# Second MLP: the lower part of the second of each two up weight tiles made by GpSimd

## The chip, the core and the metric

The kernel runs on one core of a Trainium2 chip. The metric is the device time of one execution in microseconds (us), from the core's first to its last instruction and what lies around that span; the median of several executions counts, and less is better.

The engines are named as the profile names them: PE is TensorE (matmuls), PEld its weight loads, DVE is VectorE, ACT is ScalarE, POOL is GpSimd, SP is the queue that issues the DMAs. SBUF is the on-chip memory in which all tiles lie, PSUM the banks into which matmuls accumulate.

## The reference

A trunk of two layers over 512 positions of width 1024, for one sequence, all in float32. Layer 0 is a hybrid attention mixer, layer 1 a pooling mixer; each is followed by a squared-ReLU MLP of inner width 4096, and the end is an RMSNorm. What matters here is the MLP of layer 1 and the end:

```
def squared_relu_mlp(h, w1, w2):
    return jnp.square(jax.nn.relu(h @ w1)) @ w2
...
x = x + (gate * squared_relu_mlp(h, mlp_w1[layer], mlp_w2[layer])).astype(x.dtype)
...
return rms_norm(x, final_norm_w)
```

## The kernel before, in words

**Products in parts.** Every float32 operand of a matmul is split into two parts of a shorter format: a high part (`wh`, `hh`, `gh`), which is the operand cast by ACT, and a lower part (`wl`, `hl`, `gl`), which is the operand less its high part, a subtract of 128 partitions. A product is then three matmuls (`mm3`, lines 368 to 372): high by high, high by lower, lower by high. So each weight tile is loaded by a DMA into a tile `w`, cast by ACT (line 364, `load_hi`) and subtracted (line 366). `load_hi` hands the subtract back as a function of the engine, and `load_w` calls it with its argument `lo`.

**The second MLP.** The inner width is worked through in eight chunks (0 to 7) of 512 columns, each as four blocks `f` of 128 columns. The generator `up_blocks` makes a chunk's blocks one after the other. For `f` = 0 and `f` = 2 it first loads two weight tiles of 128x1024 each: one for the first four of the eight slices of 128 rows of `w1` (`k0` = 0), one for the last four (`k0` = 4). A block is 24 matmuls of 128x512, three for each slice, in the order of the slices; two blocks share the two tiles. Then ACT takes relu and square from PSUM, and DVE makes the lower part of the result (line 418, `gl`, for a chunk of odd number). Chunk 0 and half of chunk 1 are made ahead; `up_blocks` makes the other half of chunk 1 and chunks 2 to 7, which is 13 pairs of tiles.

**Order.** Between the blocks stand the down products. Chunks are taken in pairs (0, 1), (2, 3), (4, 5) and multiplied with `w2` by a scheme of seven half-size products (class `Pair`: `begin`, `differences`, `steps`), whose sums and differences, and the splits of the `w2` tiles (lines 1606 and 1607), are work for DVE and ACT. The last pair (6, 7) is multiplied plainly (`direct`). In this part PE's order is the written one. That of ACT, DVE and POOL is decided by the scheduler when the program is built, unless the engine's name is bound to the wrapper `_InOrder`, which keeps each instruction behind those written before it. Once built, each engine runs its list in order.

Before the last blocks the engine name `V` (DVE) is bound anew:

```
V, weights = _InOrder(tc, nc.vector), []
for r in range(2):
    weights.append(pair.split(f"{r + 1}1"))
    next(blocks)
for _ in blocks:
    pass
```

At that point `blocks` is chunk 7 with its first block made. The loop splits four `w2` tiles (`split("11")`), makes block 1, splits four more (`split("21")`) and makes block 2, for which `up_blocks` first loads the last pair of weight tiles; then come block 3 and `direct`. The argument of `load_w` has a default, written before any of this:

```
def load_w(src, a, b, parts=1, lo=V, pool=None):
```

A default is bound where the function is defined: there, `V` is the engine without the wrapper.

Of the kernel before, what the change touches and what calls it, by code (L numbers as in the profile page):

```python
# [84 lines left out]
def trunk(ctx: ExitStack, tc: tile.TileContext, ins, out):  # L85
    nc = tc.nc
    V, S, G, TE = nc.vector, nc.scalar, nc.gpsimd, nc.tensor
# [20 lines left out]
    def mm_ps():  # L108
        return ps_mm.tile([P, 512], F32, tag="mm", name=nm("mm"))
# [230 lines left out]
    def load_w(src, a, b, parts=1, lo=V, pool=None):  # L340

        w, make_lo = load_hi(src, a, b, parts, pool)
        make_lo(lo)
        return w

    def load_hi(src, a, b, parts=1, pool=None):

        n = a * b
        rt = wraw.tile([P, RAW], F32, tag="raw", name=nm("w"))
        if parts == 1:  # L350
            load(rt[:, :n].rearrange("p (a b) -> p a b", a=a), src)
        else:
            dst = rt[:, :n].rearrange("p (a c b) -> p a c b", a=a, c=parts)
            for i in range(parts):
                load(dst[:, :, i], src[:, :, i])
        if pool is None:
            pool = wsplit
        if spare:
            turn[0] += 1
            if turn[0] % 6 >= 4:  # L360
                pool = spare[0]
        th = pool.tile([P, RAW], F32R, tag="wh", name=nm("wh"))
        tl = pool.tile([P, RAW], F32R, tag="wl", name=nm("wl"))
        S.copy(th[:, :n], rt[:, :n])  # L364
        w = tuple(t[:, :n].rearrange("p (a b) -> p a b", a=a) for t in (th, tl))
        return w, lambda e: e.tensor_tensor(tl[:, :n], rt[:, :n], th[:, :n].bitcast(F32), op=ALU.subtract)  # L366

    def mm3(ps, wh, wl, ah, al, start, stop):

        TE.matmul(ps, wh, ah, start=start, stop=False)  # L370
        TE.matmul(ps, wh, al, start=False, stop=False)  # L371
        TE.matmul(ps, wl, ah, start=False, stop=stop)  # L372
# [4 lines left out]
    class Mlp:  # L377
# [81 lines left out]
        def up_blocks(self, c, g, f0=0, pools=(None, None)):  # L459

            hh, hl = self.h
            for f in range(f0, 4):
                if f % 2 == 0:
                    by = []
                    for k0 in (0, 4):
                        c0 = c * FC + f * P
                        wh, wl = load_w(self.w1[:, k0 : k0 + 4, c0 : c0 + 256], 4, 256, pool=pools[f // 2])
                        by += [(wh, wl, i) for i in range(4)]
                ps = mm_ps()
                cs = slice(f % 2 * P, (f % 2 + 1) * P)  # L470
                for k in range(ND):
                    wh, wl, kk = by[k]
                    mm3(ps, wh[:, kk, cs], wl[:, kk, cs], hh[k], hl[k], k == 0, k == ND - 1)
                self.act(g, f, slice(0, T), ps)
                yield
# [129 lines left out]
    V, S, G, TE = [_InOrder(tc, e) for e in (V, S, G, TE)]  # L605
# [740 lines left out]
    V, S, G, TE = nc.vector, nc.scalar, nc.gpsimd, nc.tensor  # L1346
# [187 lines left out]
    V, S, G, TE = [_InOrder(tc, e) for e in (V, S, G, TE)]  # L1534
# [13 lines left out]
    V, S, G, TE = nc.vector, nc.scalar, nc.gpsimd, nc.tensor  # L1548
# [209 lines left out]
    TE, pools = _InOrder(tc, nc.tensor), (wsplit, wsplit2)  # L1758
# [27 lines left out]
    V, weights = _InOrder(tc, nc.vector), []  # L1786
# [43 lines left out]
```

## Time and profile before

| | |
|---|---|
| median of 3 executions | 1001.47 us (998.39 to 1001.85) |
| the profiled execution's own time | 997.38 us |
| its span, first to last instruction | 995.7 us |
| mean granted TensorE clock | 0.995 of full speed |
| PE busy | 968.0 us, 97% of the span |
| DVE busy | 675.7 us, 68% |
| ACT busy | 490.2 us, 49% |
| POOL busy | 188.0 us, 19% |

The profile is one execution. A row of the timeline gives an instruction's start and duration, and in brackets how long the engine had been idle before it and who ended that idle time. A row of a chain or a list of waits says who waited for whom. The part around the change runs from about 670 us to the last matmul at 987 us. Line numbers are those of the kernel before; L81 is the wrapper `_InOrder`, so every instruction issued through it has that line.

### The profile page before, as it was taken

To read this page: it belongs to the slowest core of one execution; us is meant where nothing else is said; L and a number is where in the kernel's file an instruction comes from. 1 tells how busy PE (TensorE), PEld (TensorE's weight loads), DVE (VectorE), ACT (ScalarE), POOL (GpSimd) and SP (SyncE) were. 2 spreads that over 40 slices of the span, in tenths; PEclk is the share of its full clock that TensorE was granted. 3 is DMA by queue.
4 is the path that set the end of the run, shared out by engine and by line. 5 is a ranking of instruction groups with operands and counts; after the bars stand their busy time and mean duration, and the time that the engine had idled before them with its cause. 6 is when DMAs were issued, how large, how long until landed. Compare 5 with 4: busy or idle time off the path is not lost.

```text
span 995.7 us, 14343 instructions
## 1 busy us (share of the span) xinstructions
PE 968.0 (97%) x5392; PEld 804.6 (81%) x5392; DVE 675.7 (68%) x1181; ACT 490.2 (49%) x913; POOL 188.0 (19%) x136
## 2 busy tenths in 40 slices
PE   6989999998999999999999999999999999999996
PEld 5568888788987778787777899998788788778885
DVE  3678886666886757666665427859557856886385
ACT  6566657665542433333343435665664544455511
POOL 0033436456120201111122345400000000000000
PEclk9999999999999999999999999999999999999999
DMA  9973566442375656465566312172451253042202
GB/s 309 339 173 106 170 188 217 154 141 64 107 240 183 221 157 214 134 208 187 170 211 207 107 49 83 60 245 78 127 169 43 85 161 93 0 152 102 74 34 84
DMA packets 119367, 145.57 MB, mean 146 GB/s; under 512 B 5782, under 2 KB 86018, under 8 KB 119298
## 3 DMA queue, kind: packets, MB, share of 16 engines
q1 hardware_dynamic: 119138, 144.59, 46.9%
q8 instruction: 42, 0.69, 0.3%
q14 instruction: 27, 0.22, 0.1%
q10 hardware_dynamic: 160, 0.07, 0.0%
HBM read 140.25 MB, written 4.39 MB: 145 GB/s over the span
## 4 chain that ended last, share of the span: by engine, by line
PE 87%; DVE 5%; issue 2%; DMA 2%; POOL 2%; ACT 1%; SPq 1%; DVEq 0%; POOLq 0%; ACTq 0%
PE mm L81 33%; PE mm L370 10%; PE sc L81 10%; PE mm L372 10%; PE mm L371 10%; PE po L81 5%; PE tp L81 5%; PE ad L81 2%; DMA adaw<-in_ada_w 1%; SPq L81 1%; DVE wl L1607 1%; POOL wl L81 1%; PE ad L283 1%; POOL sqsum L81 1%; DMA xin<-in_x 1%
## 5 line engine op out<-in xcount | busy, mean ns | idle before, releaser
L364 ACT CAST wh<-w 128x1024 fp32r<-128x1024 f32 x82 | 85.8, 1050 | 110.0 <-PE mm L371 80.2
L81 PE MATMUL mm<-hh,wl 128*128 128x512 f32 (+1 forms) x312 | 116.1, 379 | 2.0 <-DVE wl L366 2.0
L366 DVE TENSOR_TENSOR wl<-w,wh 128x1024 fp32r<-128x1024 f32 x76 | 100.0, 1320 | 24.3 <-ACT wh L364 23.2
L81 PE MATMUL mm<-hh,wh 128*128 128x512 f32 (+1 forms) x312 | 116.3, 380 | 0.0
L81 PE MATMUL mm<-hl,wh 128*128 128x512 f32 (+1 forms) x312 | 115.5, 377 | 0.0
L81 POOL TENSOR_TENSOR wl<-w,wh 128x1024 fp32r<-128x1024 f32 x36 | 87.6, 2444 | 79.9 <-ACT wh L81 77.1
L371 PE MATMUL mm<-hl,wh 128*128 128x512 f32 (+1 forms) x256 | 95.7, 376 | 0.0
L372 PE MATMUL mm<-hh,wl 128*128 128x512 f32 (+1 forms) x256 | 95.5, 375 | 0.0
L370 PE MATMUL mm<-hh,wh 128*128 128x512 f32 (+1 forms) x256 | 94.3, 377 | 0.0
L1606 ACT CAST wh<-w 128x512 fp32r<-128x512 f32 x100 | 56.9, 619 | 53.2 <-PE po L81 21.9
L370 PE MATMUL mm<-gh,wh 128*128 128x512 f32 x192 | 75.9, 395 | 0.0
L371 PE MATMUL mm<-gl,wh 128*128 128x512 f32 x192 | 74.8, 390 | 0.0
L372 PE MATMUL mm<-gh,wl 128*128 128x512 f32 x192 | 74.8, 390 | 0.0
L81 PEld LDWEIGHTS mm<-hh,wl 128*128 128x128 f32 x312 | 58.7, 188 | 15.6 <-DVE wl L366 4.0
L81 PEld LDWEIGHTS mm<-hh,wh 128*128 128x128 f32 x312 | 58.9, 189 | 11.6 <-ACT wh L364 0.6
L81 PEld LDWEIGHTS mm<-hl,wh 128*128 128x128 f32 x312 | 58.9, 189 | 11.3
L1607 DVE TENSOR_TENSOR wl<-w,wh 128x512 fp32r<-128x512 f32 x84 | 54.7, 689 | 17.7 <-ACT wh L1606 17.5
L248 DVE SCALAR_TENSOR_TENSOR acc<-adaw,sc,acc 128x512 f32<-128x512 f32 x60 | 46.7, 778 | 21.0 <-DMA adaw<-in_ada_w 20.4
L274 POOL TENSOR_TENSOR adaw<-adaw 128x512 f32<-128x512 f32 x12 | 15.7, 1306 | 232.4 <-ACT adaw L272 199.4
L375 DVE SCALAR_TENSOR_TENSOR x<-mm,mod,x 128x512 f32<-128x512 f32 x48 | 35.7, 746 | 31.8 <-PE mm L372 31.8
L81 ACT CAST wh<-w 128x1024 fp32r<-128x1024 f32 (+1 forms) x44 | 43.8, 1004 | 25.8 <-DMA w<-in_attn_w_in 9.3
L372 PEld LDWEIGHTS mm<-hh,wl 128*128 128x128 f32 x256 | 48.2, 188 | 9.6 <-issue 0.8
(499 smaller groups left out, 2488.9 us busy)
## 6 DMA issues: line engine op xcount, KB each, us to landing
w<-in_mlp_w SPq DMA_DIRECT2D x98, 512.0 KB, 4.1
adaw<-in_ada_w SPq DMA_DIRECT2D x92, 512.0 KB, 4.6
w<-in_mlp_w SPq DMA_DIRECT2D x64, 256.0 KB, 3.7
w<-in_attn_w_in SPq DMA_DIRECT2D x8, 512.0 KB, 3.6
w<-in_attn_w_out SPq DMA_DIRECT2D x8, 512.0 KB, 3.5
w<-in_attn_w_in SPq DMA_DIRECT2D x8, 392.0 KB, 7.9
xin<-in_x SPq DMA_DIRECT2D x4, 512.0 KB, 5.7
adaw<-in_ada_w SPq DMA_DIRECT2D x8, 256.0 KB, 6.1
```

What stands on the lines that cost most here:

```text
L81: return lambda *args, **kw: self.tc.keep_in_program_order(f(*args, **kw))
L248: V.scalar_tensor_tensor(acc, rv, sk, acc, op0=ALU.mult, op1=ALU.add)
L274: G.tensor_tensor(rv[:, 0], rv[:, 0], rv[:, 1], op=ALU.add)
L283: TE.matmul(ps[32 * j : 32 * j + 32], one_col[:, 31 - r : 63 - r], self.acc[:, j * P : (j + 1) * P], start=True, stop=True)
L364: S.copy(th[:, :n], rt[:, :n])
L366: return w, lambda e: e.tensor_tensor(tl[:, :n], rt[:, :n], th[:, :n].bitcast(F32), op=ALU.subtract)
L370: TE.matmul(ps, wh, ah, start=start, stop=False)
L371: TE.matmul(ps, wh, al, start=False, stop=False)
L372: TE.matmul(ps, wl, ah, start=False, stop=stop)
L375: V.scalar_tensor_tensor(x[j][:, ts], ps, g, x[j][:, ts], op0=ALU.mult, op1=ALU.add)
L1606: S.copy(th[:, cs], self.raw[key, f])
L1607: V.tensor_tensor(tl[:, cs], self.raw[key, f], th[:, cs].bitcast(F32), op=ALU.subtract)
```

## The change

For the second MLP (`pairs` is set there and only there) `up_blocks` hands the subtract of the pair's second tile to POOL; that of the first stays on DVE.

```
@@ -464,7 +464,8 @@
                     by = []
                     for k0 in (0, 4):
                         c0 = c * FC + f * P
-                        wh, wl = load_w(self.w1[:, k0 : k0 + 4, c0 : c0 + 256], 4, 256, pool=pools[f // 2])
+                        lo = G if k0 and self.pairs else V
+                        wh, wl = load_w(self.w1[:, k0 : k0 + 4, c0 : c0 + 256], 4, 256, lo=lo, pool=pools[f // 2])
                         by += [(wh, wl, i) for i in range(4)]
```

The lists of PE, ACT and SP keep their order; DVE's is 13 rows shorter and POOL's 13 longer. The places of which the prediction speaks follow. A name's last number tells one tile from another; from line 467 on a line of the changed kernel has a number one higher.

POOL, end of its list, in the changed kernel: the first 6 of 13 new rows, which stand behind all that POOL had before (its last row of work was a sum `sqsum`, at 647 us).

```order
L366 TENSOR_TENSOR wl_1112_6927<-w_1110_6924,wh_1111_6926 128x1024
L366 TENSOR_TENSOR wl_1154_7189<-w_1152_7186,wh_1153_7188 128x1024
L366 TENSOR_TENSOR wl_1174_7340<-w_1172_7337,wh_1173_7339 128x1024
L366 TENSOR_TENSOR wl_1202_7472<-w_1200_7469,wh_1201_7471 128x1024
L366 TENSOR_TENSOR wl_1228_7634<-w_1226_7631,wh_1227_7633 128x1024
L366 TENSOR_TENSOR wl_1264_7848<-w_1262_7845,wh_1263_7847 128x1024
```

Each is a subtract that stood in DVE's list; POOL has nothing else between them.

DVE at the first pair of chunk 4 (tiles 7842 and 7848), before; `sum0`, `sum1` and `x4` take up products of the pair (2, 3), `sl` is the lower part of a difference that PE multiplies next, `gp` belongs to the block's result.

```order
L1640 TENSOR_TENSOR sum0_6835<-sum0_6835,sc_1253_7805 128x512
L366 TENSOR_TENSOR wl_1261_7842<-w_1259_7839,wh_1260_7841 128x1024
L1640 TENSOR_TENSOR sum1_6836<-sum1_6836,sc_1254_7818 128x512
L1621 TENSOR_TENSOR sl_1256_7834<-gf_1148_7179,sh_1255_7833 128x1024
L366 TENSOR_TENSOR wl_1264_7848<-w_1262_7845,wh_1263_7847 128x1024
L430 TENSOR_TENSOR gp_1257_7837<-gf_1258_7838,gp_1257_7837 128x256
```

In the changed kernel the same place of DVE's list reads:

```order
L1641 TENSOR_TENSOR sum0_6835<-sum0_6835,sc_1253_7805 128x512
L366 TENSOR_TENSOR wl_1261_7842<-w_1259_7839,wh_1260_7841 128x1024
L1641 TENSOR_TENSOR sum1_6836<-sum1_6836,sc_1254_7818 128x512
L1622 TENSOR_TENSOR sl_1256_7834<-gf_1148_7179,sh_1255_7833 128x1024
L430 TENSOR_TENSOR gp_1257_7837<-gf_1258_7838,gp_1257_7837 128x256
```

Tile 7848 is gone from DVE, and nothing else has moved.

DVE at the end of chunk 7, before: the last pair's tiles are 8901 and 8907; `gl_1404` is the lower part of chunk 7's result, from block 0 (`r_1428`) and block 1 (`r_1434`); the other `wl` are the splits of `w2`.

```order
L366 TENSOR_TENSOR wl_1441_8901<-w_1439_8898,wh_1440_8900 128x1024
L366 TENSOR_TENSOR wl_1444_8907<-w_1442_8904,wh_1443_8906 128x1024
L418 TENSOR_TENSOR gl_1368_8497<-r_1402_8746,gh_1367_8496 128x512
L418 TENSOR_TENSOR gl_1404_8769<-r_1428_8839,gh_1403_8768 128x512
L81 TENSOR_TENSOR wl_1430_8845<-w2_1405_8770,wh_1429_8844 128x512
...
L81 TENSOR_TENSOR gl_1404_8769<-r_1434_8881,gh_1403_8768 128x512
L81 TENSOR_TENSOR wl_1436_8887<-w2_1409_8778,wh_1435_8886 128x512
...
L81 TENSOR_TENSOR wl_1438_8893<-w2_1412_8784,wh_1437_8892 128x512
L81 TENSOR_TENSOR gl_1404_8769<-r_1446_8935,gh_1403_8768 128x512
```

In the changed kernel the same place reads:

```order
L418 TENSOR_TENSOR gl_1368_8497<-r_1402_8746,gh_1367_8496 128x512
L418 TENSOR_TENSOR gl_1404_8769<-r_1428_8839,gh_1403_8768 128x512
L81 TENSOR_TENSOR wl_1430_8845<-w2_1405_8770,wh_1429_8844 128x512
...
L81 TENSOR_TENSOR gl_1404_8769<-r_1434_8881,gh_1403_8768 128x512
L81 TENSOR_TENSOR wl_1436_8887<-w2_1409_8778,wh_1435_8886 128x512
...
L81 TENSOR_TENSOR wl_1438_8893<-w2_1412_8784,wh_1437_8892 128x512
L81 TENSOR_TENSOR wl_1441_8901<-w_1439_8898,wh_1440_8900 128x1024
L81 TENSOR_TENSOR gl_1404_8769<-r_1446_8935,gh_1403_8768 128x512
```

Tile 8907 has gone to POOL. Tile 8901, which stays on DVE, has moved down behind both splits and behind block 1's `gl`: `V` is now read inside `up_blocks` when the pair is loaded, and there it is the wrapped engine (its row has L81). On PE block 2 of chunk 7 reads tile 8901 with its third matmul, right behind block 1.

## Rows read from the trace of the kernel before

**Rows 1.** The page's first part: engine, busy us, share of span, instructions.
```profile
PE 968.0 (97%) x5392; PEld 804.6 (81%) x5392; DVE 675.7 (68%) x1181; ACT 490.2 (49%) x913; POOL 188.0 (19%) x136
```

**Rows 2.** Who PE waited for, 560 to 996 us: total, times, longest.
```profile
PE mm L81 <- DVE wl L366: 2.0, 4, 0.5
...
PE mm L81 <- DVE gl L418: 0.7, 3, 0.2
```

**Rows 3.** Line 366 over the span: duration ns min/median/max, first and last start.
```profile
L366 DVE TENSOR_TENSOR wl<-w,wh x76: 1209/1223/2325, 266.4 to 920.5; 128x1024 fp32r<-128x1024 f32 x76
...
L366 POOL TENSOR_TENSOR wl<-w,wh x6: 2394/2402/2409, 538.3 to 566.4; 128x1024 fp32r<-128x1024 f32 x6
```

**Rows 4.** Timeline of POOL and DVE, 245 to 251 us: start, duration, instruction.
```profile
245.67 7.63 POOL L81 TENSOR_TENSOR wl<-w,wh 128x1024 fp32r<-128x1024 f32 x3
...
246.31 2.20 DVE L81 SCALAR_TENSOR_TENSOR hl<-ht,mod,hh 128x256 fp32r<-128x256 f32 x1 [0.32 <-ACT hh L81]
```

**Rows 5.** Timeline of PE, ACT and DVE, 917 to 937 us.
```profile
917.73 1.23 DVE L366 TENSOR_TENSOR wl<-w,wh 128x1024 fp32r<-128x1024 f32 x1 [2.16 <-ACT wh L364]
...
931.15 0.40 PE L81 MATMUL mm<-hh,wl 128*128 128x512 f32 x1
...
931.70 0.59 ACT L415 ACTIVATE r<-mm 128x512 f32<-128x512 f32 x1
...
933.64 0.69 DVE L81 TENSOR_TENSOR gl<-r,gh 128x512 fp32r<-128x512 f32 x1 [3.30 <-ACT r L417]
...
934.25 2.49 DVE L81 TENSOR_TENSOR wl<-w,wh 128x512 fp32r<-128x512 f32 x4
```

**Rows 6.** Windows: us, busy us (instructions) of PE, PEld, DVE, ACT, POOL, PEclk, DMA.
```profile
914.00:988.00 74.00, 73.40 (x329) 60.05 (x327) 44.13 (x78) 25.83 (x53) 0.00 (x0) 1.00 0.16 54
...
229.00:230.00 1.00, 0.00 (x0) 0.00 (x0) 0.00 (x0) 0.61 (x3) 0.92 (x2) 1.00 0.04 14
...
231.00:232.00 1.00, 1.00 (x3) 0.82 (x4) 0.11 (x1) 0.00 (x0) 1.00 (x1) 0.50 0.07 16
...
234.00:235.00 1.00, 1.00 (x9) 1.00 (x9) 0.96 (x3) 0.13 (x1) 0.00 (x0) 0.91 0.67 132
```

**Rows 7.** Timeline of DVE and PE, 675 to 697 us: chunk 1, tile 6927.
```profile
675.31 1.22 DVE L366 TENSOR_TENSOR wl<-w,wh 128x1024 fp32r<-128x1024 f32 x1
...
687.46 0.69 DVE L1607 TENSOR_TENSOR wl<-w,wh 128x512 fp32r<-128x512 f32 x1 [0.40 <-ACT wh L1606]
...
695.71 0.69 DVE L418 TENSOR_TENSOR gl<-r,gh 128x512 fp32r<-128x512 f32 x1
...
696.46 0.50 PE L81 MATMUL mm<-wh,gl 128*128 128x512 f32 x1 [0.24 <-DVE gl L418]
```

**Rows 8.** Timeline at tile 7189 (chunk 2) and at tile 7848 (chunk 4).
```profile
711.65 0.50 PE L81 MATMUL mm<-hh,wl 128*128 128x512 f32 x1 [0.53 <-DVE wl L366]
711.85 1.05 ACT L364 CAST wh<-w 128x1024 fp32r<-128x1024 f32 x1
...
795.67 1.04 ACT L364 CAST wh<-w 128x1024 fp32r<-128x1024 f32 x1
...
795.95 0.50 PE L81 MATMUL mm<-hh,wl 128*128 128x512 f32 x1 [0.53 <-DVE wl L366]
796.41 1.22 DVE L1621 TENSOR_TENSOR sl<-gf,sh 128x1024 fp32r<-128x1024 f32 x1
```

**Rows 9.** Timeline at tiles 8507 and 8660 (first and second pair of chunk 6).
```profile
880.13 1.05 ACT L364 CAST wh<-w 128x1024 fp32r<-128x1024 f32 x1
...
880.87 0.69 DVE L1755 TENSOR_TENSOR sum<-x,sum 128x512 f32<-128x512 f32 x1
...
883.89 0.50 PE L81 MATMUL mm<-hh,wl 128*128 128x512 f32 x1 [0.41 <-DVE wl L366]
...
901.66 3.13 ACT L364 CAST wh<-w 128x1024 fp32r<-128x1024 f32 x3 [1.36 <-PE po L81]
...
902.82 0.40 PE L81 MATMUL mm<-hh,wh 128*128 128x512 f32 x1
```

More of the change, by code (lines that the diff above doesn't have):

```diff
@@ L466, in up_blocks @@
                         c0 = c * FC + f * P
-                        wh, wl = load_w(self.w1[:, k0 : k0 + 4, c0 : c0 + 256], 4, 256, pool=pools[f // 2])
+                        lo = G if k0 and self.pairs else V
+                        wh, wl = load_w(self.w1[:, k0 : k0 + 4, c0 : c0 + 256], 4, 256, lo=lo, pool=pools[f // 2])
                         by += [(wh, wl, i) for i in range(4)]
```

## Prediction

> **What bounds the kernel now.** The page's first part comes first [rows 1]: PE is busy 97% of the span, POOL 19%. The windows narrow that to the stretch of the change: from 914 to 988 us PE is busy 73.40 of 74 us, and the rest is the end, after its last matmul [rows 6]. So the path that sets the end runs through PE, and a change there counts only by what it does to PE's waits. The list of waits shows how little there is to win: from 560 us on PE waits 2.0 us for line 366, in four pieces of at most 0.5, and 0.7 us for line 418 [rows 2]. If the change took away every one of these, it would give 2.7 us, 0.3% of the time, and a measurement of this kernel can't tell less than about 0.5% (5 us) from no change. What it can cost has no such lid: a tile that comes late stops PE for as long as it is late.
>
> **What the change takes and adds.** Thirteen subtracts of 128x1024 go from DVE to POOL. On DVE one takes 1.22 us and on POOL 2.40 us, both medians over whole groups [rows 3]. DVE loses 13 x 1.22 = 15.9 us of work, POOL gains 13 x 2.40 = 31.2 us in a stretch where it had none: its last such subtract began at 566.4 us [rows 3]. No matmul, cast or DMA is added or moved. POOL frees a raw tile some 1.2 us later than DVE did, and the load that goes into it is issued that much later; each such load feeds a cast some 10 us away or more, so I cost that at nothing (without that cover, 1.2 us a time).
>
> Two things decide what this does to PE: when the second tile is ready, and whether DVE can work beside POOL.
>
> **DVE beside POOL.** In the timeline from 245.67 us POOL has three such subtracts in a row, 7.63 us for 3 x 2.40 = 7.20 [rows 4]. The first ends near 248.07. DVE starts an instruction with two SBUF operands at 246.31, of a quarter of the elements, and it takes 2.20 us, to 248.51 [rows 4]: it got nowhere until POOL was done. So I count a POOL subtract as 2.40 us in which DVE can't do that kind of work, and POOL as waiting for the end of such a DVE instruction if that came first. The Trainium skill (SBUF — State Buffer, section "Who interferes with whom") speaks against the change here: a VectorE instruction with two SBUF inputs and a GpSimd instruction that reads SBUF shut each other out for the whole instruction, whichever comes first. The trace agrees, with the 2.20 us above.
>
> **Seven places where the second tile, or DVE, comes late.** A block's matmuls start 0.233 us apart in the timeline, 24 in 5.60 us (over 914 to 988 us it is 73.40 us for 329 recorded ones, 0.223, a few of them smaller [rows 6]). A block's third matmul is the first to read a lower part, and the one that reads the second tile's comes 12 later, 12 x 0.233 = 2.80 us. I allow 0.08 us from the cast's end to POOL and 0.05 from POOL's end to PE.
>
> - Tile 7189: PE took up the first tile at 711.65, so it wants the second at 714.45. The cast ends at 711.85 + 1.05 = 712.90 [rows 8]; POOL runs from 712.98 to 715.38, PE goes on at 715.43. **1.0 us.**
> - Tile 7848: wanted at 795.95 + 2.80 = 798.75. The cast ends at 796.71, but DVE holds an instruction with two SBUF operands from 796.41 to 797.63 [rows 8]; POOL from 797.63 to 800.03, PE at 800.08, against about 798.8 now. **1.2 us.** Were POOL not held up, 799.24, or 0.4.
> - Tile 8507: PE takes it at 883.89 now, after 0.41 us of waiting. The cast ends at 881.18, a DVE instruction at 881.56 [rows 9]; POOL to 883.96. **0.1 us**, or 1.2 if DVE's next instruction gets in first.
> - Tile 8660: block begun at 902.82, wanted 14 x 0.233 = 3.27 us later, at 906.09. Its cast is the second of the three from 901.66, ended by 903.75 [rows 9]; DVE, which takes the first tile when the first of these casts is done (902.71), holds POOL up to about 904.0; POOL to 906.4. **0.4 us.** The same pattern, three casts in a row, stands in chunks 2 and 4; there it gives 0.3 each. **0.6 us.**
> - Tile 6927 is in time (PE wants it over 3 us later), but here DVE is the late one. It works almost without a break from this subtract at 675.31 to the `gl` at 695.71 that PE waits for at 696.46; the one pause is 0.40 us [rows 7]. It loses 2.40 us to POOL, saves the 1.22, and has 0.40 of slack. **0.8 us.**
> - The other six second tiles are wanted 5 us or more after POOL can have them, and where POOL stands in DVE's way DVE is idle for 3 us soon after: nothing.
>
> Together 1.0 + 1.2 + 0.1 + 0.4 + 0.6 + 0.8 = **4.1 us**. If the two engines could work side by side, it would be 1.0 + 0.4 - 0.2 (tile 8507 sooner than now) + 0.2 + 0.5 + 0 = 1.9; if DVE got in first at tile 8507, 5.2. These are the bounds. By the skill's rule it is the 4.1, without it the 1.9.
>
> **The tile that moved: the largest term.** The order of DVE's list shows something that the words of the change don't say. The first tile of the last pair, 8901, is still DVE's, but it is now issued through the wrapper that keeps the written order, behind both splits and behind the `gl` of chunk 7's block 1. Before, DVE did it at 917.73, long ahead; PE reads it at 931.15 [rows 5]. In the new order it must wait for that `gl`, which waits for ACT's activations of block 1. These can't start until block 1 is done; they begin at 931.70, and `gl` at 933.64 [rows 5]. Four split subtracts follow, from 934.25, 0.60 us apart [rows 5]; the fifth in line is tile 8901, from 936.65 to 937.87. PE goes on near 937.93. **PE stands still for 6.8 us.** Nothing covers it: PE's list has only two more matmuls ahead of that one, and all that is late afterwards hangs on PE. From there to the last matmul PE has no pause that could take the delay up [rows 6], so it reaches the end whole. I see no bound that lets it shrink by more than the few tenths between instructions.
>
> **The clock.** In the row for 229 to 230 us PE did nothing, and in that for 231 to 232 its granted clock is 0.50, the lower level of 1.2 GHz in place of 2.4; at 234 to 235 it is back at 0.91 [rows 6]. So a pause of under 3 us was followed by about 3.2 us at half speed. After one of 6.8 us I expect the same: 3.2 us at half speed lose **1.6 us**; the bounds are 0 and 3.2 (twice as long).
>
> **The sum.** 4.1 + 6.8 + 1.6 = 12.5 us slower. The profiled execution took 997.38 us, 1.7 outside its span of 995.7, so it would take 1009.9. It was faster than the median of 1001.47 by 4.1 us, and the median is what counts: 1001.47 + 12.5 = **1014.0 us**.
>
> **The rivals.**
> - Only the moved tile counts: POOL's tiles come in time after all, because casts earlier in ACT's list or shorter gaps give them the lead that they lack. For it: four of the seven places are under half a microsecond. Against it: at 711.65 and 795.95 the second cast ends only 1.5 and 2.0 us before the tile is wanted, and POOL takes 2.40. Time: 1001.47 + 6.8 + 1.6 = 1009.9 us.
> - Not slower: the moved tile finds cover. That is so if DVE reaches it by 931.15 us, 6.8 earlier than in my count, which needs the `gl` ahead of it not to hang on block 1. For it: from 914 to 988 us DVE is idle 40% of the time [rows 6]. Against it: the printed order, and the activation at 931.70. Then only the seven places are left, 1.9 to 4.1 us: 1003.4 to 1005.6 us, which a measurement doesn't tell from no change.
> - The relief of DVE wins: 15.9 us fewer, all 2.7 us of waits gone, nothing late: 998.8 us. Against it: at 711.65 and 795.95 PE waits for a pair's first tile, 0.53 us each [rows 8], and that tile's way through ACT and DVE is unchanged.
>
> That the change doesn't do what it says is excluded by POOL's list, which has the thirteen rows.
>
> **How the numbers follow.** The forecast (moved tile, late POOL tiles, clock) has 0.75, its own range being 6.8 + 1.9 to 6.8 + 5.2 + 3.2 over the median, 1010 to 1017. Only the moved tile: 0.13. Not slower: 0.09. Relief: 0.03. Faster by over 0.5% would need more than relief can give, save for the spread of the runs: 0.03. Within 0.5%: the third case and a piece of the relief: 0.09. Slower by over 0.5%: 0.88. The range goes down to 1005, which takes in the second case measured against the fastest run shown (998.39 + 6.8 = 1005.2), and up to 1018, a us more than the first, for the spread of the runs.
>
> **What would show it.** In the new profile: a wait of PE for DVE's `wl` of L81 of 6 to 7 us, near 940 us, the DVE row before it being four splits; granted clock 0.50 for a few microseconds just after; waits of PE for POOL's `wl` of L366 of about 1 us at the first pair of chunks 2 and 4; DVE instructions of twice their length beside POOL's. I am wrong if that long wait is missing (the third rival), or if PE's waits for POOL add up to under 1 us (the first).

## The result, and the profile after

The changed kernel takes **1014.79 us** (median of 4 runs, 1014.24 to 1016.06); the kernel before, on the same chip, 1001.29 us. The ratio is 1.0149, with a 95% interval of 1.0127 to 1.0171: 1.5% slower. The predicted time was 1014.0 us. The profiled execution of the changed kernel took 1014.97 us, its span was 1013.2 us.

The page's first part after the change, against [rows 1]:

```profile
PE 974.2 (96%) x5392; PEld 807.6 (80%) x5392; DVE 671.8 (66%) x1168; ACT 490.0 (48%) x913; POOL 222.0 (22%) x149
```

POOL has 13 instructions more and 34.0 us more work, DVE 13 instructions fewer and only 3.9 us less. Thirteen subtracts of 1.22 us would be 15.9: much of the other 12 us is DVE instructions drawn out beside POOL (rows below have 4.11 us in place of 1.89, and 3.42 in place of 1.22). The busy share of an engine hides this: it counts the waiting as work. Both differences are rough to some 2 us: e2 below, in which both engines do exactly the work of the kernel before, has 678.0 and 185.9 us for DVE and POOL, where the kernel before has 675.7 and 188.0.

Who PE waited for from 560 us on, against [rows 2] (total, times, longest):

```profile
PE mm L81 <- DVE wl L81: 6.7, 1, 6.7
PE mm L81 <- POOL wl L366: 2.5, 6, 0.9
PE mm L81 <- DVE wl L366: 1.6, 3, 0.5
PE mm L81 <- DVE gl L418: 1.3, 3, 0.8
PE po L81 <- DVE hl L81: 0.9, 1, 0.9
```

Two lines are new: one wait of 6.7 us, and six for POOL. The wait for `gl` has grown by 0.6 us, and of four waits for DVE's line 366 three are left. The last line stands in the list before too, with the same numbers. The long one, in the timeline of PE, ACT and DVE from 937 to 947 us, against [rows 5]:

```profile
939.12 0.40 PE L81 MATMUL mm<-hl,wh 128*128 128x512 f32 x1
939.94 0.59 ACT L415 ACTIVATE r<-mm 128x512 f32<-128x512 f32 x1
...
941.88 0.69 DVE L81 TENSOR_TENSOR gl<-r,gh 128x512 fp32r<-128x512 f32 x1 [3.34 <-ACT r L417]
942.50 3.62 DVE L81 TENSOR_TENSOR wl<-w,wh 128x512 fp32r<-128x512 f32 x5
...
946.17 0.79 PE L81 MATMUL mm<-hh,wl 128*128 128x512 f32 x1 [6.65 <-DVE wl L81]
```

After two matmuls of block 2 PE stands still, at 939.12 + 0.40. DVE itself is idle for 3.34 us, until ACT has made block 1's result; then come `gl` and five subtracts, which the view shows as one row. Four of them are the splits of `w2`, the fifth is tile 8901, for which PE waits. The windows of one microsecond around it (us, busy us and instructions of PE, PEld, DVE, ACT and POOL, then PEclk, the granted clock, and the DMA):

```profile
940.00:941.00 1.00, 0.00 (x0) 0.00 (x0) 0.00 (x0) 0.97 (x3) 0.00 (x0) 1.00 0.00 0
941.00:942.00 1.00, 0.00 (x0) 0.00 (x0) 0.12 (x1) 0.82 (x2) 0.00 (x0) 0.75 0.00 0
942.00:943.00 1.00, 0.00 (x0) 0.00 (x0) 1.00 (x2) 0.00 (x0) 0.00 (x0) 0.50 0.00 0
...
950.00:951.00 1.00, 1.00 (x3) 0.74 (x3) 0.00 (x0) 0.00 (x0) 0.00 (x0) 0.50 0.00 0
951.00:952.00 1.00, 1.00 (x4) 0.83 (x3) 0.00 (x0) 0.00 (x0) 0.00 (x0) 0.63 0.00 0
952.00:953.00 1.00, 1.00 (x6) 0.78 (x6) 0.00 (x0) 0.00 (x0) 0.00 (x0) 1.00 0.00 0
```

The clock falls to 0.50, 1.2 GHz, during the pause, and it is still there when PE is at work again. A row between the levels is a mean: 0.63 says that the low level filled 0.74 of that microsecond, so it ended near 951.74. (The x of a window counts every matmul that has a part in it, 3 to 4 there and later 6; fewer begin in it.) The pace is read from PE's timeline:

```profile
946.76 0.63 PE L81 MATMUL mm<-hh,wh 128*128 128x512 f32 x1
...
951.46 0.53 PE L81 MATMUL mm<-hh,wl 128*128 128x512 f32 x1
```

Between these two starts lie eleven steps, so a step takes 4.70 / 11 = 0.427 us, where 0.233 is usual at the full clock. A microsecond of work at the low clock therefore loses 1 - 0.233 / 0.427 = 0.45 us.

The other places, each in PE's timeline:

```profile
701.36 0.50 PE L81 MATMUL mm<-wh,gl 128*128 128x512 f32 x1 [0.79 <-DVE gl L418]
...
719.20 0.39 PE L81 MATMUL mm<-hl,wh 128*128 128x512 f32 x1
720.29 0.50 PE L81 MATMUL mm<-hh,wl 128*128 128x512 f32 x1 [0.70 <-POOL wl L366]
720.62 0.39 PE L81 MATMUL mm<-hh,wh 128*128 128x512 f32 x1
...
742.82 0.50 PE L81 MATMUL mm<-hh,wl 128*128 128x512 f32 x1 [0.18 <-POOL wl L366]
...
806.18 0.50 PE L81 MATMUL mm<-hh,wl 128*128 128x512 f32 x1 [0.90 <-POOL wl L366]
...
828.74 0.50 PE L81 MATMUL mm<-hh,wl 128*128 128x512 f32 x1 [0.19 <-POOL wl L366]
...
891.66 0.50 PE L81 MATMUL mm<-hh,wl 128*128 128x512 f32 x1 [0.39 <-POOL wl L366]
...
914.20 0.50 PE L81 MATMUL mm<-hh,wl 128*128 128x512 f32 x1 [0.18 <-POOL wl L366]
```

The three rows around 720 us show how to price a wait. From the start of one matmul to the start of the second after it takes 720.62 - 719.20 = 1.42 us, where two steps of 0.233 are usual: 0.95 us lost, of which the list calls 0.70 a wait. A new wait costs some 0.26 us more than its entry in the list, since that counts from the end of the matmul before (its row overlaps the next one's) and the first matmul behind the pause is slower.

**A ledger that leaves out what differs ahead of the change.** How long the kernel takes up to chunk 1 differs from run to run: the matmul that waits for `gl` there starts at 696.46 us in the trace before [rows 7], at 701.36 in this one, at 696.77 to 702.47 in the others. All but the wait itself arose before the change acts. So I compare what comes behind: from the start of that matmul to the end of the span, plus what its own wait has grown. Each row rests on one profiled execution; e3 and e6, where nothing but that wait should differ, come within 0.1 us of it.

| kernel | start | span | rest | change of rest, with the wait at the start |
|---|---|---|---|---|
| before | 696.46 | 995.7 | 299.2 | |
| the change | 701.36 | 1013.2 | 311.8 | +12.6 + 0.55 = **+13.2** |
| e1, POOL only | 698.31 | 1000.8 | 302.5 | +3.3 + 0.55 = **+3.8** |
| e2, moved tile only | 700.90 | 1008.6 | 307.7 | **+8.5** |
| e3, six late tiles | 700.27 | 999.4 | 299.1 | **-0.1** |
| e4, filled pause | 700.79 | 1010.3 | 309.5 | +10.3 + 0.55 = **+10.8** |
| e5, ahead of the split | 702.47 | 1011.0 | 308.5 | +9.3 + 0.55 = **+9.8** |
| e6, tile 6927 only | 701.05 | 1000.3 | 299.2 | 0.0 + 0.56 = **+0.6** |
| e7, halves | 696.77 | 994.5 | 297.7 | **-1.5** |
| e8, the change again | 698.84 | 1010.6 | 311.8 | +12.5 + 0.56 = **+13.1** |

The prediction's sum was 12.5.

### The profile page after: what moved, and what is told of

Its sections match the earlier page's. It is cut to its first block, busy times and chain, and to the rows that moved or that the text cites. A ratio compares the mean times of both kernels' runs of the same rounds, so it can differ in the third digit from the quotient of the medians.

```text
span 1013.2 us, 14351 instructions
## 1 busy us (share of the span) xinstructions
PE 974.2 (96%) x5392; PEld 807.6 (80%) x5392; DVE 671.8 (66%) x1168; ACT 490.0 (48%) x913; POOL 222.0 (22%) x149
## 5 line engine op out<-in xcount | busy, mean ns | idle before, releaser
L81 PE MATMUL mm<-hh,wl 128*128 128x512 f32 (+1 forms) x312 | 118.1, 386 | 10.8 <-DVE wl L81 6.7
L81 PE MATMUL mm<-hh,wh 128*128 128x512 f32 (+1 forms) x312 | 117.5, 384 | 0.0
L81 PE MATMUL mm<-hl,wh 128*128 128x512 f32 (+1 forms) x312 | 116.9, 382 | 0.0
L366 POOL TENSOR_TENSOR wl<-w,wh 128x1024 fp32r<-128x1024 f32 x19 | 49.4, 2606 | 275.5 <-ACT wh L364 171.8
L81 POOL TENSOR_TENSOR wl<-w,wh 128x1024 fp32r<-128x1024 f32 x36 | 87.3, 2434 | 82.7 <-ACT wh L81 76.9
L366 DVE TENSOR_TENSOR wl<-w,wh 128x1024 fp32r<-128x1024 f32 x62 | 81.6, 1320 | 20.3 <-ACT wh L364 19.3
L81 PEld LDWEIGHTS mm<-hh,wl 128*128 128x128 f32 x312 | 59.7, 191 | 26.8 <-DVE wl L81 7.1
L81 PEld LDWEIGHTS mm<-hh,wh 128*128 128x128 f32 x312 | 59.9, 192 | 11.7 <-ACT wh L364 0.6
L81 PEld LDWEIGHTS mm<-hl,wh 128*128 128x128 f32 x312 | 59.7, 191 | 11.6
```

The source lines that it names most:

```text
L81: return lambda *args, **kw: self.tc.keep_in_program_order(f(*args, **kw))
```

## The experiments

The theory: three costs add up, the places where a second tile or DVE is late, the pause for tile 8901, and the clock after it. Each was taken out or made alone.

**e1: POOL's tiles without the moved one.** The first tile takes the default of the argument again, so the list of DVE is the changed kernel's but for tile 8901, which is back in its old place.

```
-                        lo = G if k0 and self.pairs else V
-                        wh, wl = load_w(..., 4, 256, lo=lo, pool=pools[f // 2])
+                        lo = {"lo": G} if k0 and self.pairs else {}
+                        wh, wl = load_w(..., 4, 256, pool=pools[f // 2], **lo)
```

> Thirteen second tiles on POOL as in the change, but the first tile takes the default of its argument again, so tile 8901 stands in its old place in DVE's list. Theory A (places, moved tile and clock add up): the long stall and the half-speed stretch are gone and the seven places are left, about 4.0 us slower than before (3.3 to 5.0), a third of the change's loss; in the trace six waits of PE for POOL's line 366, 2.5 us together, the longest 0.9 at tile 7848, none over 1.5 us for DVE's wl, granted clock 1.00 from 914 to 988 us. Rival B (only the moved tile counts): within 1 us of before. Rival C (POOL as a whole is the cost, the moved tile finds cover): close to the change, 11 us or more slower than before.

Measured: 1004.0 us against 999.46 before, ratio 1.0041 (1.0025 to 1.0058), so 2.5 to 5.8 us; 3.8 by the ledger. The list of PE's waits has the six for POOL (2.6 us, the longest 0.9) and the 0.8 for `gl`, and no long one; the granted clock from 914 to 988 us is 1.00. Rivals B and C fall: POOL's tiles cost something that can be measured, and they are under a third of the whole.

**e2: the moved tile without POOL.** Only the first tile is handed `V` at the call; the second stays on DVE.

```
-                        lo = G if k0 and self.pairs else V
-                        wh, wl = load_w(..., 4, 256, lo=lo, pool=pools[f // 2])
+                        lo = {} if k0 else {"lo": V}
+                        wh, wl = load_w(..., 4, 256, pool=pools[f // 2], **lo)
```

> POOL gets nothing; only the last pair's first tile is issued through the wrapper, so tiles 8901 and 8907 stand behind both splits and block 1's gl in DVE's list. Theory A: one wait of PE for wl of 6.6 to 6.7 us (6.9 with the restart of the matmuls), then about 5 us at half speed that lose 2.6 us: 9.5 us slower than before (8.5 to 10.5). As predicted with the clock at 1.6: 8.4. Rival C (the stall comes from POOL, which holds DVE up near its subtracts): a wait of 4 us or less and at most 5 us slower. Tile 8907, right behind 8901, is ready 1.2 us after it and wanted 2.8 us after it: no second wait.

Measured: 1008.83 us, ratio 1.0095 (1.0080 to 1.0111), 8.5 by the ledger. PE's timeline:

```profile
942.36 0.80 PE L81 MATMUL mm<-hh,wl 128*128 128x512 f32 x1 [6.61 <-DVE wl L81]
```

The pause is the same without any work on POOL, so rival C (POOL makes it) falls. The windows at both ends of the low clock:

```profile
939.00:940.00 1.00, 0.00 (x0) 0.00 (x0) 1.00 (x3) 0.00 (x0) 0.00 (x0) 0.60 0.00 0
...
946.00:947.00 1.00, 1.00 (x6) 0.82 (x5) 0.00 (x0) 0.00 (x0) 0.00 (x0) 0.98 0.00 0
```

It ended near 946.04 here, 3.7 us after PE resumed, where it was 5.6 in the changed kernel. By the ratios e1 and e2 together make 1.36%; the change, run beside other kernels as e8, 1.37%. By the ledger they make 12.3 us against e8's 13.1: after e2's pause the low clock lasted 1.5 us less, which is worth 0.7.

**e3: only the tiles that are wanted late.** The six second tiles of chunks 3, 5 and 7 go to POOL, tile 8901 keeps its place.

```
+                        lo = {"lo": G} if k0 and self.pairs and c % 2 and c > 1 else {}
```

> Only the six second tiles that are wanted late go to POOL (both pairs of chunks 3, 5 and 7); tile 8901 keeps its place. Theory A: no wait of PE for POOL, within 0.5 us of before, though POOL works 14.5 us beside DVE. Rival D (POOL's lock on DVE costs wherever it works): up to 2.4 us for each, several us slower. Rival E (DVE's relief counts): up to 2.7 us faster, the waits for DVE's line 366 shorter than 0.5 us.

Measured: 998.99 us, ratio 0.9994 (0.9981 to 1.0007). PE's waits from 660 us on are those of before [rows 2], to the digit:

```profile
PE mm L81 <- DVE wl L366: 2.0, 4, 0.5
PE mm L81 <- DVE gl L418: 0.7, 3, 0.2
```

So a subtract on POOL cost nothing at these six, whose tiles are wanted late and where the prediction found a gap of DVE's soon after; no run takes the two conditions apart. Nothing is gained either: taking these six off DVE is worth nothing to PE, and D and E both fall.

**e4: the pause filled.** The change, with 28 matmuls ahead of block 2 whose result nobody reads.

```
     for r in range(2):
         weights.append(pair.split(f"{r + 1}1"))
+        if r == 1:
+            ps, hh = ad_ps(), mlp1.h[0]
+            for i in range(28):
+                TE.matmul(ps, hh[i % ND][:, 0:P], hh[i % ND], start=i == 0, stop=i == 27)
         next(blocks)
```

> The change, with 28 more matmuls of 128x512 into a bank that nobody reads, written between block 1 and block 2 of chunk 7, so that PE works through the time in which tile 8901 is late. Theory A (the half-speed stretch follows from the pause): a wait of about 0.4 us for DVE's wl of L81 is left (6.65 less 28 x 0.223), granted clock 1.00 throughout, and 2.6 us are won back: 10.9 us slower than before, 1012.2 us by the median, against 13.5 for the change. Rival F (the clock falls there for another reason): half speed as in the change, 13 us slower or more.

Measured: 1012.15 us, ratio 1.0127 (1.0109 to 1.0146). The median lies between what the theories expected, and its interval ends at the 10.9 us of A, so the time alone settles little; the windows over the pause do:

```profile
939.00:946.00 7.00, 6.72 (x30) 5.20 (x30) 4.24 (x6) 2.27 (x4) 0.00 (x0) 1.00 0.00 0
946.00:952.00 6.00, 6.00 (x27) 4.87 (x26) 0.00 (x0) 0.89 (x2) 0.00 (x0) 1.00 0.02 3
```

The clock stays at 1.00, and the wait for tile 8901 is 0.28 us. In the ledger it costs 10.8, the change 13.2 and 13.1: without the low clock 2.3 to 2.4 us are saved. So the half-speed stretch comes from the pause and is a cost of its own. F falls. The medians show less of it, 12.7 us over before where e8 has 13.6. In e4's profiled execution what comes ahead of the change took 3.8 us longer than in the trace before, which the ledger leaves out; for the other executions there is no trace.

**e5: the tile ahead of the second split.** The last pair is loaded right behind block 1, so that in DVE's list tile 8901 stands behind block 1's `gl`, ahead of `split("21")`; the other lists are the same.

```
+                if f == 1 and c == NFC - 1 and self.pairs:
+                    early = pair_of(2)
                 yield
```

(`pair_of` is the body of the loop over `k0`; block 2 of chunk 7 takes `early`.)

> The change, with the last pair of weight tiles loaded just after block 1 of chunk 7 instead of just before block 2: in DVE's list tile 8901 then stands behind split(11) and block 1's gl, but ahead of the four subtracts of split(21); nothing else moves. Theory A (the stall is the sum of what stands ahead of tile 8901 in DVE's list): the long wait loses just these four, 2.49 us of the timeline, and is 6.65 - 2.4 = 4.2 us (4.1 to 4.4); the time is 4.0 + 4.5 + 1 to 2.8 for the clock = 9.5 to 11.3 us over before. Rival G (what counts is the wait for the activations alone): the wait stays at 6.6. Rival H (being issued through the wrapper at all): it stays at 6.6 too.

Measured: 1009.56 us, ratio 1.0097 (1.0077 to 1.0117), 9.8 by the ledger. PE's timeline:

```profile
944.99 0.80 PE L81 MATMUL mm<-hh,wl 128*128 128x512 f32 x1 [4.25 <-DVE wl L81]
```

6.65 less 4.25 is 2.40 us, four splits at 0.60: what no longer stands ahead of the tile in DVE's list is gone from the pause. G and H fall. The low clock ended near 948.20, 3.2 us after PE resumed:

```profile
948.00:949.00 1.00, 1.00 (x5) 0.77 (x5) 0.00 (x0) 0.00 (x0) 0.00 (x0) 0.90 0.00 0
```

**e6: one tile on POOL.** Only tile 6927 (chunk 1), with `c == 1` in the condition of e3 in place of its last two.

> Only the second tile of chunk 1, 6927, goes to POOL; the rest is the kernel before. Theory A (DVE and POOL shut each other out during a subtract): a DVE row of three splits beside POOL's subtract takes 4.1 us instead of 1.89, and the wait of PE for block 3's gl, some 20 us later, is 0.79 us instead of 0.24; no wait of PE for POOL. Rival I (they work side by side): no DVE row longer than without POOL, the wait for gl at most 0.24.

One execution, 1001.98 us; what counts are two rows. DVE's timeline has three of `w2`'s differences beside POOL's subtract, and PE's the wait some 20 us later:

```profile
678.74 4.11 DVE L1614 TENSOR_TENSOR w<-w,w 128x512 f32<-128x512 f32 x3
...
701.05 0.50 PE L81 MATMUL mm<-wh,gl 128*128 128x512 f32 x1 [0.80 <-DVE gl L418]
```

Three such instructions take 1.89 us elsewhere (756.77 us in the changed kernel). Here the first did not get on until POOL was done: 2.22 us lost. PE waits 0.80 instead of 0.24 [rows 7], and nowhere for POOL. The Trainium skill (SBUF — State Buffer, section "Who interferes with whom") says that the two engines shut each other out in this case; the trace agrees, with the 4.11 us. I falls.

**e7: a version that beats both.** The kernel before, with the subtracts of the first pair of chunks 2, 4 and 6 in two halves, so that PE can begin on the first.

```
+        cuts = [slice(i * n // halves, (i + 1) * n // halves) for i in range(halves)]
-        return w, lambda e: e.tensor_tensor(tl[:, :n], rt[:, :n], th[:, :n].bitcast(F32), op=ALU.subtract)
+        return w, lambda e: [e.tensor_tensor(tl[:, s], rt[:, s], th[:, s].bitcast(F32), op=ALU.subtract) for s in cuts]
...
+                        kw = {"halves": 2} if self.pairs and c % 2 == 0 and f == 0 else {}
```

> The kernel before, all on DVE, but with the subtracts of the first pair of chunks 2, 4 and 6 each made in two halves of 128x512, so that PE can take up the first two slices after 0.69 us instead of 1.22. Theory A (PE waits for the end of these subtracts, and each wait that goes also saves 0.26 us of restart): the 0.53 us waits for the first tiles vanish; the second tiles of chunks 4 and 6 are then waited for, 0.4 to 0.7 us; in sum 1.6 us faster than before (0.8 to 2.4). Rival J (the cast, not the subtract, ends last): no change.

Measured: 998.2 us against 999.81, ratio 0.9983 (0.9970 to 0.9995), 1.5 us by the ledger. PE's waits (its line numbers are one higher):

```profile
PE mm L81 <- DVE gl L419: 0.7, 3, 0.2
PE mm L81 <- DVE wl L367: 0.5, 1, 0.5
```

The three waits of 0.53 for a first tile are gone from the list, but not whole. PE's timeline at the first of them:

```profile
711.06 0.40 PE L81 MATMUL mm<-hl,wh 128*128 128x512 f32 x1
711.45 0.50 PE L81 MATMUL mm<-hh,wl 128*128 128x512 f32 x1
711.78 0.39 PE L81 MATMUL mm<-hh,wh 128*128 128x512 f32 x1
```

Two steps take 0.72 us, 0.25 more than usual: the tile is still a little late, too little for the list, and the first matmul behind it is slow again. So each place gives back some 0.53, not the 0.79 that I had expected. One wait is left, 0.48 at the second tile of chunk 6; that of chunk 4, which I had expected too, is not in the list. The two misses cancel, so that the 1.6 expected was met by luck as to its parts. It is the fastest version of the study, by 0.2%.

**e8: the change again**, on the chip of e5 to e7.

> The change itself once more, on the chip of the runs beside it. Theory A: 13 us over before (11.5 to 14.5), the same seven places, a wait of 6.65 us for tile 8901; the stretch at half speed after it anywhere between 3.7 us (as in the run that only moves the tile) and 5.6 us (as in the changed kernel's profile), so 1.8 to 2.8 us lost.

Measured: 1013.39 us, ratio 1.0137 (1.0118 to 1.0156), 13.1 by the ledger, with the same waits (6.66 for tile 8901). By the windows (0.51 from 942 us, 0.58 from 948 us, 0.50 between) the low clock lasted from about 942.02 to 948.84 us, of which PE, resuming at 943.68, worked 5.2 us.

## Why the prediction was right

It was right in time and in mechanism, and each of its terms has now been seen by itself; one of them, the clock, was sized too small.

**The seven places, 4.1 us predicted.** A new wait is its entry in the list plus 0.26:

| tile | predicted | measured in the changed kernel |
|---|---|---|
| 6927 (through DVE) | 0.8 | 0.79 - 0.24 = 0.55 |
| 7189 | 1.0 | 0.70 + 0.26 = 0.96 |
| 7340 | 0.3 | 0.18 + 0.26 = 0.44 |
| 7848 | 1.2 | 0.90 + 0.26 = 1.16 |
| 7999 | 0.3 | 0.19 + 0.26 = 0.45 |
| 8507 | 0.1 | 0.39 - 0.41 = -0.02 |
| 8660 | 0.4 | 0.18 + 0.26 = 0.44 |
| sum | 4.1 | 3.98 (e1 as a whole: 3.8) |

The two large ones were right for the reasons given. At tile 7848 the rows of POOL and DVE in the changed kernel are:

```profile
802.68 1.22 DVE L1622 TENSOR_TENSOR sl<-gf,sh 128x1024 fp32r<-128x1024 f32 x1
...
803.11 3.02 POOL L366 TENSOR_TENSOR wl<-w,wh 128x1024 fp32r<-128x1024 f32 x1 [42.20 <-issue]
```

POOL is ready at 803.11 and held until DVE's subtract ends at 803.90; 2.23 us later it is done, at 806.13, and PE goes on at 806.18. Tile 6927 was priced too high: DVE lost 2.22 us to POOL (e6), not 2.40. With 1.22 saved and 0.40 of slack that leaves 0.60, and 0.55 was seen. At the three small tiles (7340, 7999, 8660) the prediction was a little low, and the errors cancel in the sum. At tile 8507 it took 0.1 us over the 1.2 of the other order without working out which would come; the lower one did.

**The moved tile, 6.8 us predicted.** 6.65 in the changed kernel, 6.61 and 6.66 in e2 and e8, 6.9 with the restart. e5 shows that it is made of the instructions ahead in DVE's list, e2 that POOL has no part in it. It is half of the loss, and the words of the change don't mention it: it comes of naming `V` at the call, where the default had caught the engine without the wrapper.

**The clock, 1.6 us predicted.** This term was too small in the changed kernel. Its step was "After one of 6.8 us I expect the same: 3.2 us at half speed". The length was wrong: a pause of 6.65 us was followed by 5.6 us at the low clock, and in e8 by 5.2. So was, slightly, what a microsecond costs: 0.45 us and not 0.5, by the steps of 0.427 and 0.233. That makes 2.5 us in the changed kernel and 2.3 in e8, and comparing the ledger with e4 gives 2.4 and 2.3. After the same pause e2 had 3.7 us, and after 4.25 us e5 had 3.2, worth 1.7 and 1.4; the ledger, less the pause with its restart (and in e5 less the 3.8 of e1), leaves 1.6 and 1.5. So the one stretch before did not carry a length (it was itself 3.4 us, counted from 230.77, where PE came back); the bounds, 0 to 3.2 us lost, held.

**The sum.** 4.0 + 6.9 + 2.5 is 13.4, where the ledger has 13.2 and 12.5 was predicted; without the clock it is 10.9, and e4 has 10.8. So the forecast was short by 0.7 us, nearly all of it in the clock's term. By the medians the loss is 13.5.

**The rivals.** "Only the moved tile" is excluded by e1. "Not slower" needed the long wait to be missing (the prediction's last lines call it the third rival; it is the second of its list): the wait is there. "The relief of DVE wins" is excluded by e1, in which all thirteen are off DVE and the kernel is slower, with PE's waits of 0.5 us for DVE's line 366 still there; e3, with six of them off, leaves PE's waits as they were.

## What to carry to other kernels

Read the order of each engine's list, not only the diff: a default that is now spelled out can bind another object, and here that cost as much as all the rest. Before work is moved to a slower engine, ask for each tile when its reader wants it; the same edit was free for six tiles and cost up to 1.2 us each at others. When the engine that sets the end waits for a large instruction, halving that instruction can be worth more than moving it: here moving by itself lost 0.4% (e1), and halving six subtracts gave 0.2% (e7).

## What the runs showed of the hardware

**Who gets in first beside POOL is not settled by who asked first.** Rows of DVE and POOL in the changed kernel, chunks 5 and 6:

```profile
843.28 1.89 DVE L1614 TENSOR_TENSOR w<-w,w 128x512 f32<-128x512 f32 x3
845.09 0.42 DVE L430 TENSOR_TENSOR gp<-gf,gp 128x256 fp32r<-128x256 f32 x1
...
843.36 4.40 POOL L366 TENSOR_TENSOR wl<-w,wh 128x1024 fp32r<-128x1024 f32 x1 [12.33 <-ACT wh L364]
...
889.28 3.42 DVE L1622 TENSOR_TENSOR sl<-gf,sh 128x1024 fp32r<-128x1024 f32 x1
...
889.11 2.50 POOL L366 TENSOR_TENSOR wl<-w,wh 128x1024 fp32r<-128x1024 f32 x1 [41.35 <-issue]
```

At 843.36 POOL comes just after DVE's first instruction, and three more of DVE's go ahead of it: DVE is done at 845.51, POOL 2.25 us later. The same happens at 757.45 us, where POOL comes 0.08 us after the second of three such instructions: the third goes ahead, and POOL's subtract takes 3.47 us. At 889.11 POOL comes during another DVE instruction (a sum of 0.69 us that began at 888.67) and gets in ahead of DVE's next one, which takes 3.42 us instead of 1.22. The prediction had allowed for both at tile 8507 (0.1 or 1.2 us). The Trainium skill (SBUF — State Buffer, section "Who interferes with whom") says that the order of issue decides who blocks; the row at 889.11 agrees, that at 843.36 does not: there instructions of DVE that came later went ahead. What decides between them stays open; no run was made for it.

**The low clock differs after the same pause.** After pauses of 6.61 to 6.66 us PE worked 3.7, 5.2 and 5.6 us at 1.2 GHz, after one of 4.25 us it worked 3.2, and with the pause filled none. Each of these microseconds cost 0.45 us. From such rows the share in the loss can be bounded before a run, but not told to the microsecond.
